# Attention's projected blocks in another order, and the last six units of the last pattern interleaved differently on TensorE

## The chip, the core and the metric

The kernel runs on one core of one Trainium2 chip. The metric is the device time of one execution in microseconds (us). A core has a matrix engine (TensorE, PE in the profile, with its weight loads as PEld), a vector engine (VectorE, DVE), a scalar engine (ScalarE, ACT), GpSimd (POOL) and a queue engine (SyncE, SP) from which most DMA transfers are issued. Each engine works through its own instruction queue in order; semaphores tie the queues together.

## The reference, cut to what matters

A trunk of two layers on 1024 tokens of width 1024: attention and a gated feed-forward network, then an RWKV-7 time mix and another feed-forward network. Only the attention of the first layer is touched. It projects the normed tokens to sliding-window heads (12 query heads on 3 key/value heads, window 128, with a sink) and to three dilated patterns of 4 heads each:

```python
proj = h @ w_in + b_in
qa, ka, va, qb, kb, vb = jnp.split(proj, IN_SPLITS, axis=-1)
qa = rope_partial(...); ka = rope_partial(...)
out_a, _ = banded_attention(qa, ka, va, A_WINDOW - 1, sinks)
for gi, (win, dil) in enumerate(((128, 1), (512, 4), (2048, 16))):
    o, l = dilated_attention(qb[:, :, gi], kb[:, :, gi], vb[:, :, gi], win, dil)
wts = jax.nn.softmax(jnp.stack(lses), axis=0)
out_b = jnp.sum(wts[..., None] * jnp.stack(outs), axis=0)
return jnp.concatenate([out_a, out_b], axis=-1) @ w_out
```

`banded_attention` takes blocks of 128 queries, each against its own and the block before, with a softmax. In the last pattern a block of 128 queries sees only its own 128 keys.

## The kernel before

Every float32 product is done as three matmuls on a value split into a high and a low part (`split`, `load_split`, `mm3`, lines 149 to 176): ACT casts the high part, DVE subtracts it to get the low part, both at line 154.

The projection is cut into 24 blocks of 128 output columns, listed in `PROJ` (line 41): `ak01` and `ak2` are the keys of the sliding heads (two, and the third), `aq`, `q`, `k`, `v` with a group number 0 to 2 and a pair number 0 or 1 are queries of the sliding heads and queries, keys and values of the patterns. A block is done in two halves of 512 tokens. `project` runs one half: 8 steps of 3 matmuls (24 matmuls of 128x512), handing control back after the third, the sixth and the last step. A half ends in an eviction: `rotated` (rotary embedding through ACT, DVE, POOL and DVE), `window_keys`, or `values` (an ACT eviction to `vT`, line 360, whose transposes on PE are put in the list `late` and done later by `transpose_values`, with an ACT copy to `vt`, line 350).

The attention itself is cut into 48 units, a unit being 128 queries of 4 heads: 8 units for each of the windows 0, 1, 2 (`window`) and of the patterns 0, 1, 2 (`pattern`). A unit (`unit`, line 439 on) has three steps. Step 0: scores (PE, line 454, tiles `sc`), the mask with the row minimum (DVE, line 458) and four exponentials (ACT, line 466) into the tile `pr`; the windows also divide by the sum there (DVE and POOL, line 473). Step 1: transposes on PE (line 481, tiles `tr`) and two ACT copies to `pT` (line 483). Step 2: values times probabilities on PE (line 490, one PSUM tile `pv`) and a DVE copy into the output tile (line 492: `oa` for the windows, `ob` for the patterns). The scores use two PSUM tiles for one unit, so the next unit's scores wait for this unit's DVE pass.

The order on PE is written out by hand: `seen` chains every one of these matmuls to the one before. The loop of lines 538 to 552 goes through the 48 half-blocks. In each it starts one unit if the block number has reached that unit's number in `todo` (step 0 ahead of the matmuls, the unit before gets its step 1 after the first part and its step 2 after the second) and does one pending value transpose behind each of these. With the numbers of before, unit steps begin at the ninth half-block, so that 40 units start within the loop and the 8 units of pattern 2 are left. What is left runs in a second loop (lines 553 to 560), two deep: the scores of one unit, then steps 1 and 2 of the unit before. The queues of the other engines are laid out by the scheduler that builds the program.

After each four units of a window its `oa` tile is written to memory (`oT`, line 528); after a pattern's last unit its `ob` goes to `oB` (line 506) and its sums to `st`. `oT` is read back (`oraw`, line 622) into the buffers of the projection's weights and split (line 154, tiles `o`) into the memory of the normed tokens `hx`, so these casts wait for the last matmuls that read `hx`. Then `out_proj` loads `wout` (line 167), while `merge` reads `oB` (tiles `om`, line 606) and weighs the patterns.

Of the kernel before, what the change touches and what calls it, by code (L numbers as in the profile page):

```python
# [11 lines left out]
F32 = mybir.dt.float32  # L12
# [9 lines left out]
P = 128  # L22
# [5 lines left out]
H = 512  # L28
# [9 lines left out]
VNAMES = ["nm0", "nf0", "nm1", "nf1", "mu0", "mu1", "mu2", "mu3", "mu4", "mu5", "w0", "a0", "kk", "ka", "rk", "lb"]  # L38
VI = {n: i for i, n in enumerate(VNAMES)}

PROJ = ["ak01", "ak2"] + [f"{n}{i}{pr}" for n, i in (("aq", 0), ("k", 0), ("q", 0), ("aq", 1), ("k", 1), ("v", 1), ("q", 1), ("aq", 2),
                                                     ("k", 2), ("v", 2), ("q", 2)) for pr in range(2)]
NV = 448


# [34 lines left out]
def lay_out(inp):  # L80
# [16 lines left out]
    for p in range(3):  # L97
        for pr in range(2):
            for n, c in (("aq", 0), ("q", 1152), ("k", 1920), ("v", 2688)):
                sl[f"{n}{p}{pr}"] = two(c + 256 * p + P * pr)  # L100
    o["win"] = np.stack([w[:, sl[n]].reshape(NK, P, P).transpose(1, 0, 2).reshape(P, NK * P) for n in PROJ])
    o["bin"] = np.stack([b[sl[n]] for n in PROJ], 1)
    v0 = np.concatenate([np.arange(2688, 2944), np.arange(960, 1152)])
# [19 lines left out]
class Trunk:  # L123
# [137 lines left out]
    def attention(self, hp, mp):  # L261
# [82 lines left out]
        late = []  # L344
# [81 lines left out]
        ap = pool("ap", 2)  # L426
# [12 lines left out]
        def unit(q, kT, keys, mask, vs, stat, sink, dst):  # L439
# [5 lines left out]
            n = keys.stop - keys.start  # L445
# [1 line left out]
            nm, den = stat if stat else (ap.tile([P, 4], F32, name=n_, tag=n_, bufs=6) for n_ in ("am", "ad"))  # L447

            ss = [psum.tile([P, 2, 256], F32, name="sc", tag="sc") for _ in range(2)]
            p = ap.tile([P, 4, 256], F32, name="pr", tag="pr", bufs=2)  # L450
            for pr in range(2):
                for e in range(2):
                    r = slice(e * 64, e * 64 + 64)
# [62 lines left out]

        def window(j, b, state):
            if b % 4 == 0:
                state[:] = [ap.tile([P, 2, H], F32, name="oa", tag="ol", bufs=2)]
            os_ = state[0]  # L520
            kb = [0] if b == 0 else [b - 1, b]
            yield from unit([qw[j][:, pr, b * P:(b + 1) * P] for pr in range(2)], [kTA[:, j]] * 2, slice(kb[0] * P, (b + 1) * P),
                            maskA[:, P:] if b == 0 else maskA, [[vtA[:, i, j * 64:(j + 1) * 64]] * 4 for i in kb], None,
                            slice(4 * j, 4 * j + 4), os_[:, :, b % 4 * P:(b % 4 + 1) * P])
            if b % 4 == 3:
                q = b // 4
                for pr in range(2):
                    nc.sync.dma_start(oT[2 * j + pr][:, q * H:(q + 1) * H], os_[:, pr])
            yield
# [1 line left out]


        todo = []
        for of, j, n in ((window, 0, 4), (pattern, 0, 8), (window, 1, 10), (pattern, 1, 16), (window, 2, 18), (pattern, 2, 24)):
            state = []
            todo += [(of(j, b, state), n) for b in range(NB)]
        before = None
        for at in range(2 * len(PROJ)):
            i = at // 2
            if at % 2 == 0 and 2 <= i + 1 < len(PROJ):  # L540
                weights(i + 1)
            mm = project(i, at % 2, seen)
            here = todo.pop(0)[0] if todo[0][1] <= i else None
            for part in range(3):
                if here and part == 0:
                    next(here)
                if before and part:
                    next(before)
                if late and part:
                    transpose_values(*late.pop(0))  # L550
                next(mm)
            before = here
        for here, _ in [*todo, (None, 0)]:
            if here:
                next(here)
            if late:
                transpose_values(*late.pop(0))
            for _ in range(2):
                next(before)
            before = here  # L560
        ev = mp.tile([P, 8, 3, 4], F32, name="ev")
        selr = mp.tile([44, 6 * P], F32R, name="selr")
        two = (slice(0, 12), slice(32, 44))
# [1068 lines left out]
```

## Time and profile before

| what | us |
|---|---|
| median of three runs (lowest, highest) | 2867.52 (2865.66, 2872.91) |
| the profiled execution | 2867.93 |
| its span, first to last instruction | 2866.2 |
| busy PE, DVE, ACT, POOL | 2674.2, 1789.1, 1204.6, 1099.7 |
| loop over the half-blocks, about 90 to 463.6 | 373.6, PE busy 371.25 |
| the units after it, 463.6 to 513.7 | 50.1, PE busy 31.95 |
| from there to the first matmul of the output projection | 12.8, PE busy 0 |

Times in the trace count from the first instruction of the span. The execution's own time is 1.7 us longer than its span. PE is busy for 93% of the span as a whole, but not in every stage, so a stage is read from the rows of its own stretch: how busy each engine is there, the clock that was granted to PE (1.00 is full speed), and what ended each idle time of PE.

### The profile page before, as it was taken

To read this page: it belongs to the slowest core of one execution; us is meant where nothing else is said; L and a number is where in the kernel's file an instruction comes from. 1 tells how busy PE (TensorE), PEld (TensorE's weight loads), DVE (VectorE), ACT (ScalarE), POOL (GpSimd) and SP (SyncE) were. 2 spreads that over 40 slices of the span, in tenths; PEclk is the share of its full clock that TensorE was granted. 3 is DMA by queue.
4 is the path that set the end of the run, shared out by engine and by line. 5 is a ranking of instruction groups with operands and counts; after the bars stand their busy time and mean duration, and the time that the engine had idled before them with its cause. 6 is when DMAs were issued, how large, how long until landed. Compare 5 with 4: busy or idle time off the path is not lost. (4 is left out here: it accounts for less than half of the span.)

```text
span 2866.2 us, 38024 instructions
## 1 busy us (share of the span) xinstructions
PE 2674.2 (93%) x13302; PEld 2135.3 (75%) x13302; DVE 1789.1 (62%) x3017; ACT 1204.6 (42%) x2377; POOL 1099.7 (38%) x830
## 2 busy tenths in 40 slices
PE   8999997799999999998899889888899999999998
PEld 6777775577888877786577667777787888887776
DVE  4555555457444437798667888767676544444988
ACT  3445444234333334355544454434334433333334
POOL 1221211136443424545444433334643534431644
PEclk9999997799999999999999999789999999999999
DMA  4111111452222227462446366787743222225654
GB/s 138 38 45 46 45 51 46 150 191 78 83 82 78 85 94 263 151 207 78 154 138 166 98 212 163 195 216 208 208 162 129 89 89 77 85 70 184 217 155 162
DMA packets 301536, 367.18 MB, mean 128 GB/s; under 512 B 101000, under 2 KB 175112, under 8 KB 301344
## 3 DMA queue, kind: packets, MB, share of 16 engines
q1 hardware_dynamic: 296560, 351.08, 39.5%
q10 hardware_dynamic: 4496, 12.62, 1.1%
q8 instruction: 105, 1.72, 0.3%
q0 software_dynamic: 288, 1.05, 0.1%
q14 instruction: 87, 0.71, 0.1%
HBM read 268.98 MB, written 95.68 MB: 127 GB/s over the span
## 5 line engine op out<-in xcount | busy, mean ns | idle before, releaser
L910 PE MATMUL pd<-ws,as 128*128 128x512 f32 x1848 | 435.7, 397 | 19.9 <-DVE ws L154 18.8
L910 PEld LDWEIGHTS pd<-ws,as 128*128 128x128 f32 x1848 | 353.5, 192 | 100.0 <-DVE ws L154 23.9
L762 PE MATMUL y<-t,cw 128*128 128x512 f32 x1584 | 370.2, 389 | 0.0
L762 PEld LDWEIGHTS y<-t,cw 128*128 128x128 f32 x1584 | 297.3, 188 | 62.4
L154 DVE TENSOR_TENSOR cw<-raw,cw 128x512 fp32r<-128x512 f32 x264 | 214.5, 815 | 197.2 <-ACT cw L154 195.9
L154 ACT CAST cw<-raw 128x512 fp32r<-128x512 f32 x264 | 163.4, 621 | 242.5 <-PE z L762 102.3
L154 ACT CAST wh<-raw 128x512 fp32r<-128x512 f32 (+1 forms) x154 | 119.8, 780 | 202.5 <-PE mm L174 58.4
L154 DVE TENSOR_TENSOR wl<-raw,wh 128x512 fp32r<-128x512 f32 (+1 forms) x146 | 144.0, 988 | 95.2 <-ACT wh L154 94.9
L771 POOL TENSOR_TENSOR c<-c 128x512 f32<-128x512 f32 x66 | 111.4, 1688 | 188.1 <-DVE c L778 137.0
L173 PE MATMUL mm<-hx,wh 128*128 128x512 f32 x384 | 163.3, 425 | 0.0
L766 ACT COPY sn<-y 128x512 f32<-128x512 f32 x132 | 77.0, 588 | 196.4 <-PE y L762 193.1
L175 PE MATMUL mm<-hx,wl 128*128 128x512 f32 x384 | 152.3, 397 | 0.0
L174 PE MATMUL mm<-hx,wh 128*128 128x512 f32 x384 | 151.6, 395 | 0.0
L762 PE MATMUL z<-b,cw 128*128 128x512 f32 x576 | 141.6, 396 | 6.6 <-DVE tx L708 6.6
L257 POOL TENSOR_TENSOR ry<-ry,S 128x512 f32<-128x512 f32 x40 | 52.0, 1301 | 222.5 <-DVE ry L256 198.0
L154 ACT CAST as<-raw 128x512 fp32r<-128x512 f32 x110 | 68.3, 621 | 157.4 <-PE pd L910 82.3
L762 PEld LDWEIGHTS z<-b,cw 128*128 128x128 f32 x576 | 110.2, 192 | 30.8 <-issue 7.0
L762 PE MATMUL y<-b,cw 128*128 128x512 f32 x528 | 129.0, 394 | 0.0
L762 PE MATMUL z<-t,cw 128*128 128x512 f32 x528 | 123.3, 389 | 0.0
L804 POOL TENSOR_TENSOR raw<-s,raw 128x512 f32<-128x512 f32 x44 | 59.9, 1362 | 152.8 <-DVE cw L154 152.6
L762 PE MATMUL x<-b,cw 128*128 128x512 f32 x480 | 117.4, 400 | 0.0
L154 DVE TENSOR_TENSOR as<-raw,as 128x512 fp32r<-128x512 f32 x110 | 100.0, 909 | 27.4 <-ACT as L154 27.3
(469 smaller groups left out, 6122.5 us busy)
## 6 DMA issues: line engine op xcount, KB each, us to landing
raw<-act SPq DMA_DIRECT2D x132, 256.0 KB, 3.5
raw<-in_wd SPq DMA_DIRECT2D x132, 256.0 KB, 3.3
raw<-in_wg SPq DMA_DIRECT2D x88, 256.0 KB, 2.9
raw<-in_wu SPq DMA_DIRECT2D x88, 256.0 KB, 2.5
act<-c SPq DMA_DIRECT2D x88, 256.0 KB, 2.0
raw<-in_wrk SPq DMA_DIRECT2D x32, 512.0 KB, 4.6
raw<-in_win SPq DMA_DIRECT2D x24, 512.0 KB, 3.3
raw<-in_wout SPq DMA_DIRECT2D x32, 256.0 KB, 3.8
```

Of the source, the lines that this page charges most:

```text
L154: return self.nc.scalar.copy(hi, src), (eng or self.nc.vector).tensor_tensor(lo, src, hi.bitcast(F32), SUB)
L173: seen(mm(ps, lh, rh, start=start, stop=False))
L174: seen(mm(ps, lh, rl, start=False, stop=False))
L175: seen(mm(ps, ll, rh, start=False, stop=stop))
L257: nc.gpsimd.tensor_tensor(y, y, self.S[:, s], MUL)
L762: seen(pe.matmul(ps, w[:, x, s], bs[:, k, y], start=start and k == j == 0, stop=k == 3 and j == 2, skip_group_check=True))
L766: ac.copy(s, ps)
L771: po.tensor_tensor(g, g, u, MUL)
L804: po.tensor_tensor(a11, s, a11, SUB)
L910: pe(ps[b], s[:, x, t], w[:, y], start=first and i == 0, stop=f == N - 1 and i == 2, skip_group_check=True)
```

## The change

Three things change. `PROJ` has another order: `ak2` comes just ahead of window 2's queries instead of second, and `v2` behind `q2`. The numbers in `todo` follow it: window 0 starts at block number 3, counted from 0 (the seventh half-block), and two units of pattern 2 start in the last two half-blocks, so that 42 units start in the loop and 6 are left; the last half-block skips its step 2. The remaining units run three deep: a turn has the scores of unit u, step 2 of unit u-3 and step 1 of unit u-2 (unit 0 gets its step 2 in the first turn). To hold this, `pr` has three buffers instead of two, and `oa` one instead of two. Because `v2` is now the last block, the transposes of its second pair fall behind the loop.

```diff
-PROJ = ["ak01", "ak2"] + [f"{n}{i}{pr}" for n, i in (("aq", 0), ("k", 0), ("q", 0), ("aq", 1), ("k", 1), ("v", 1), ("q", 1), ("aq", 2),
-                                                     ("k", 2), ("v", 2), ("q", 2)) for pr in range(2)]
+two_of = lambda *names: [f"{n}{pr}" for n in names for pr in range(2)]
+PROJ = ["ak01", *two_of("aq0", "k0", "q0", "aq1", "k1", "v1", "q1"), "ak2", *two_of("aq2", "k2", "q2", "v2")]
...
-            p = ap.tile([P, 4, 256], F32, name="pr", tag="pr", bufs=2)
+            p = ap.tile([P, 4, 256], F32, name="pr", tag="pr", bufs=3)
...
-                state[:] = [ap.tile([P, 2, H], F32, name="oa", tag="ol", bufs=2)]
+                state[:] = [ap.tile([P, 2, H], F32, name="oa", tag="ol", bufs=1)]
...
-        for of, j, n in ((window, 0, 4), (pattern, 0, 8), (window, 1, 10), (pattern, 1, 16), (window, 2, 18), (pattern, 2, 24)):
+        for of, j, n in ((window, 0, 3), (pattern, 0, 7), (window, 1, 11), (pattern, 1, 15), (window, 2, 19), (pattern, 2, 23)):
...
-                if before and part:
+                if before and (part == 1 or part == 2 and at + 1 < 2 * len(PROJ)):
                     next(before)
...
+            last_two = before, here
             before = here
-        for here, _ in [*todo, (None, 0)]:
-            if here:
-                next(here)
-            if late:
+
+        live = [[u, n] for u, n in zip(last_two, (2, 1))] + [[u, 0] for u, _ in todo]
+
+        def step(u, n):
+            if 0 <= u < len(live) and live[u][1] == n:
+                next(live[u][0])
+                live[u][1] += 1
+
+        for u in range(2, len(live) + 3):
+            step(u, 0)
+            while late:
                 transpose_values(*late.pop(0))
-            for _ in range(2):
-                next(before)
-            before = here
+            step(u - 3, 2)
+            step(u - 2, 2)
+            step(u - 2, 1)
```

How it moves instructions is seen at two places. The first is TensorE behind the last projection matmul. `sc` are scores, `tr` transposes of probabilities, `tq` transposes of values, `pv` the products with the values (`vtA` the windows', `vt` the patterns'). Before:

```order
L454 MATMUL sc<-kT,q 128x128 x4
L481 MATMUL tr<-cst,pr 128x128 x8
L490 MATMUL pv<-pT,vtA 64x128 x8
L454 MATMUL sc<-kT,q 128x128 x4
L481 MATMUL tr<-cst,pr 128x128 x4
L490 MATMUL pv<-pT,vt 64x128 x4
```

And with the change:

```order
L454 MATMUL sc<-kT,q 128x128 x4
L349 MATMUL tq<-cst,vT 128x128 x8
L490 MATMUL pv<-pT,vt 64x128 x4
L454 MATMUL sc<-kT,q 128x128 x4
L481 MATMUL tr<-cst,pr 128x128 x4
L454 MATMUL sc<-kT,q 128x128 x4
L490 MATMUL pv<-pT,vt 64x128 x4
L481 MATMUL tr<-cst,pr 128x128 x4
L454 MATMUL sc<-kT,q 128x128 x4
L490 MATMUL pv<-pT,vt 64x128 x4
```

The last window unit's transposes and products have moved into the loop, two groups of value transposes have come out of it, and the transposes of a unit now stand two scores behind its own, with a further unit's scores between them and their products.

The second place is ScalarE at the same time, from the casts of the window outputs (`o<-oraw`) on. Before:

```order
L154 CAST o<-oraw 128x512 x6
L254 ACTIVATE rx<-mm,bias 128x512
L154 CAST o<-oraw 128x512 x4
L466 ACTIVATE pr,stat<-pr,stat 128x128 x4
L483 COPY pT<-tr 128x512 x2
L466 ACTIVATE pr,stat<-pr,stat 128x128 x3
L483 COPY pT<-tr 128x256
L466 ACTIVATE pr,stat<-pr,stat 128x128
L483 COPY pT<-tr 128x256
L154 CAST o<-oraw 128x512 x2
```

And with the change:

```order
L154 CAST o<-oraw 128x512 x6
L360 ACTIVATE vT<-mm,bias 128x64x8
L154 CAST o<-oraw 128x512 x3
L350 COPY vt<-tq 128x4x128
L154 CAST o<-oraw 128x512
L466 ACTIVATE pr,stat<-pr,stat 128x128 x4
L154 CAST o<-oraw 128x512 x2
L350 COPY vt<-tq 128x4x128
L466 ACTIVATE pr,stat<-pr,stat 128x128
L483 COPY pT<-tr 128x256
L466 ACTIVATE pr,stat<-pr,stat 128x128
L483 COPY pT<-tr 128x256
```

The eviction of the last value block and its two copies now stand among the twelve casts, ahead of the first exponentials of the remaining units; all twelve casts stand ahead of the first copy of `pT` there.

More of the change, by code (lines that the diff above doesn't have):

```diff
@@ L551, in attention @@
                 next(mm)
+            last_two = before, here
             before = here
-        for here, _ in [*todo, (None, 0)]:
-            if here:
-                next(here)
-            if late:
+        live = [[u, n] for u, n in zip(last_two, (2, 1))] + [[u, 0] for u, _ in todo]
[6 more added lines that the diff above has]
+            while late:
                 transpose_values(*late.pop(0))
-            for _ in range(2):
-                next(before)
-            before = here
+            step(u - 3, 2)
+            step(u - 2, 2)
+            step(u - 2, 1)
+        assert all(n == 3 for _, n in live)
         ev = mp.tile([P, 8, 3, 4], F32, name="ev")
```

## The prediction

> **What bounds the kernel now.** I read the granted clock in the page's slices first, then the time by stretch, then TensorE's rows around the weakest stretch.
>
> ```profile
> PEclk9999997799999999999999999789999999999999
> ```
>
> Each digit is a fortieth of the span, 71.7 us. Slices seven and eight (430 to 573) are the weakest. The change lies there, so I cut that time into the loop over half-blocks, the units behind it, and the wait for the output projection. The columns are the length, the busy time of PE, PEld, DVE, ACT and POOL with counts, the granted clock, the DMA share and GB/s.
>
> ```profile
> 90.00:463.60 373.60, 371.25 (x2239) 278.29 (x2238) 203.71 (x643) 178.86 (x499) 79.47 (x60) 1.00 0.14 46
> 463.60:513.70 50.10, 31.95 (x185) 20.80 (x184) 22.41 (x88) 23.50 (x91) 2.40 (x3) 0.57 0.11 33
> 513.70:526.50 12.80, 0.00 (x0) 0.00 (x0) 2.98 (x11) 0.90 (x2) 1.70 (x4) 0.50 0.90 274
> ```
>
> The loop is PE-bound: 2.35 us idle in 373.6. Behind it no engine is: 50.1 us in which PE is busy for 31.95 at 0.57 of its clock, ACT for 23.5, DVE for 22.4. That is a chain of waits, and PE's rows show which.
>
> ```profile
> 472.57 0.80 PE L454 MATMUL sc<-kT,q 64*128 64x128 f32 x4 [8.47 <-DVE q L333]
> ...
> 483.52 1.11 PE L481 MATMUL tr<-cst,pr 128*128 128x128 f32 x4
> ...
> 505.58 1.34 PE L490 MATMUL pv<-pT,vt 128*64 128x128 f32 x8 [1.00 <-ACT pT L483]
> 506.85 1.23 PE L454 MATMUL sc<-kT,q 64*128 64x128 f32 x8
> 508.01 1.11 PE L481 MATMUL tr<-cst,pr 128*128 128x128 f32 x4
> 510.12 1.35 PE L490 MATMUL pv<-pT,vt 128*64 128x128 f32 x8 [1.00 <-ACT pT L483]
> 511.40 1.12 PE L481 MATMUL tr<-cst,pr 128*128 128x128 f32 x4
> 512.55 1.12 PE L490 MATMUL pv<-pT,vt 128*64 128x128 f32 x8
> 526.51 0.79 PE L173 MATMUL po<-wh,o 128*128 128x512 f32 x1 [12.84 <-ACT wh L154]
> ```
>
> First 8.47 us wait for the rotated `q` of the very last block. Then each unit takes 4.54 us (505.58 to 510.12): scores 1.16, transposes about 1.1, a wait, products 1.28, all at half clock. At the end 12.84 us until the first weights of the output projection are split.
>
> **The change, part by part.**
>
> *The wait for `q` goes.* `q2` now ends at half-block 44 and the two first units of pattern 2 start at 47 and 48. The last block is `v2`, which no score reads.
>
> *The loop grows.* It takes in two score steps, one four-matmul transpose step and the last window unit's steps 1 and 2, and gives up the two transpose groups of the last value pair. Full-clock prices:
>
> ```profile
> 457.33 1.04 PE L481 MATMUL tr<-cst,pr 128*128 128x128 f32 x8
> 458.12 0.48 PE L173 MATMUL mm<-hx,wh 128*128 128x512 f32 x1
> ...
> 460.40 0.66 PE L490 MATMUL pv<-pT,vtA 128*64 128x128 f32 x8
> 461.42 0.66 PE L490 MATMUL pv<-pT,vtA 128*64 128x128 f32 x8 [0.36 <-ACT pT L483]
> 462.01 0.50 PE L173 MATMUL mm<-hx,wh 128*128 128x512 f32 x1
> 462.34 0.39 PE L174 MATMUL mm<-hx,wh 128*128 128x512 f32 x1
> 462.57 0.39 PE L175 MATMUL mm<-hx,wl 128*128 128x512 f32 x1
> ```
>
> Eight transposes take 0.79 (457.33 to 458.12), a window's products 1.25 (460.40 to 462.01 less 0.36), scores half of 1.16. So 2 x 0.58 + 0.40 + 0.79 + 1.25 - 2 x 0.40 = 2.8 us. The distance between a block's rotation and its first reader elsewhere is as before or longer, so I put no new stall there; up to one more 2.35 us as bound.
>
> *The units behind the loop.* With three deep, a unit's exponentials have a whole turn of PE's to run in, and ACT's queue becomes the longest work. Its prices:
>
> ```profile
> 461.27 3.22 ACT L154 CAST o<-oraw 128x512 fp32r<-128x512 f32 x6
> 473.79 0.40 ACT L466 ACTIVATE pr<-pr,stat 128x128 f32<-128x128 f32 x1 [5.85 <-DVE stat L458]
> 475.35 1.04 ACT L483 COPY pT<-tr 128x512 f32<-128x512 f32 x2
> 480.69 0.35 ACT L483 COPY pT<-tr 128x256 f32<-128x256 f32 x1
> 480.94 0.40 ACT L466 ACTIVATE pr<-pr,stat 128x128 f32<-128x128 f32 x1
> 483.64 1.25 ACT L154 CAST o<-oraw 128x512 fp32r<-128x512 f32 x2 [1.96 <-DMA oraw<-oT]
> ```
>
> ```profile
> L360 ACT ACTIVATE vT<-mm,bias 128x512 f32<-128x512 f32 x8 | 9.4, 1174 | 6.6 <-PE mm L175 6.6
> ```
>
> Four exponentials take 1.56 (473.79 to 475.35), a cast 0.54 (3.22 for six), a 512-wide copy 0.52 (1.04 for two), two 256-wide copies 0.6 (0.25 and 0.35), the eviction of `vT` 1.17. Let E be the end of the last projection matmul. The first six casts wait for the last reader of half of `hx`, 12 matmuls of 0.23 before E: they run from E-2.8 to E+0.4. Then, in the built order: eviction of `vT` to 1.6, three casts 3.2, first `vt` copy 3.7, cast 4.2, unit 2's exponentials 5.8, two casts 6.9, second `vt` copy 7.4. The value transposes on PE wait for these (one `tq` tile), so PE stands idle some 3 of the first 4 us. From there each of units 3 to 7, counted from 0, brings its exponentials and the copies of the unit two before it, 1.56 + 0.6 = 2.16: 18.2. Behind that are the products of unit 5 (half a window's, 0.6), then for units 6 and 7 transposes 0.4, copies 0.6 and products 0.6 at full clock: E+22.0. DVE had a little less to do than ACT in this stretch (22.41 against 23.50), so it does not set the end. This is the lower bound.
>
> The upper bound is PE at half clock, never waiting from 3.7 on: 1.1 for the second value transposes, five scores at 1.16, five transposes at 1.11, five products at 1.28, so 22.6; then unit 5's products with the copy ahead of them 1.5 and two last pairs of 2.27 (511.40 to 513.67): E+28.6.
>
> Which one depends on the granted clock. These stretches are each as long as the shortest one at full clock, 484.86 to 488.27; the columns are PE's busy time, the clock and the DMA share, and the last two are from a later stage:
>
> ```profile
> 478.03:481.45 3.42, 2.47 (x16) 0.50 0.40 153
> 481.45:484.86 3.41, 3.19 (x20) 0.53 0.47 154
> 484.86:488.27 3.41, 0.62 (x6) 0.97 0.00 0
> ```
>
> ```profile
> 1996.95:2000.36 3.41, 1.66 (x15) 1.00 0.82 236
> 2000.36:2003.78 3.42, 2.22 (x26) 1.00 0.74 246
> ```
>
> Busy for 0.62 of 3.41, PE falls to half; busy for 2.47, it stays there; after 3.19 it rises; and once up, 1.66 of 3.41 (49%) did not lower it. So the idle start probably drops the clock, but at half clock PE is then busy without a gap, which raises it within two such stretches, by about E+10, and from there the 1.6 us that a unit takes at full clock (0.58 + 0.40 + 0.63) in each 2.16 (74%) hold it. While it is low, ACT is behind anyway. I take E+23.0, near ACT's end.
>
> ```profile
> 478.43 0.80 SPq L528 DMA_DIRECT2D oT<-oa  x2
> 480.52 0.90 SPq L622 DMA_DIRECT2D oraw<-oT  x2
> ...
> 520.64 0.99 SPq L167 DMA_DIRECT2D raw<-in_wout  x2
> ```
>
> *The read-back.* All window outputs are now written before E; before, the last went out at 478.43, was read back at 480.52 and made ACT wait 1.96 at 483.64.
>
> ```profile
> raw<-in_win SPq DMA_DIRECT2D x19, 512.0 KB, 3.3
> oB<-ob POOLq DMA_DIRECT2D x2, 512.0 KB, 6.3
> ```
>
> *The 12.84 us behind the tail.* SP's queue reads `st`, then `om`, then loads `wout`; the fourth `om` waits for POOL's two writes of the last `ob`, 6.3 us, which share the DMA engines (0.90 busy) with three `om` reads. Now the last unit's sums are ready two drain pairs before the end, so these reads go out before the writes begin. Between nothing and 3.0 (6.3 against 3.3 for one such transfer alone) I take 1.7, since two writes still share.
>
> **Sum.** +2.8 (loop) + 23.0 - 50.1 (units) - 1.7 (weights) = -26.0 against the profiled 2867.93, which is 0.4 above the median 2867.52: 2841.9, and 2841.5 beside the median. I say 2842. Ends: 2.8 + 22.0 - 50.1 - 3.0 = -28.3, so 2839.6; 2.8 + 2.35 + 28.6 - 50.1 = -16.3, so 2851.6. What follows is serial on the attention's result and PE-bound, so it shifts.
>
> **The rivals.**
>
> *The clock stays low to the end:* E+28.6, so 2867.9 + 2.8 + 28.6 - 50.1 - 1.7 = 2847.5. For it: the tail of before never stayed up. Against: there PE had about 1 us of idle in each stretch (3.42 - 2.47), and here it would have none. The Trainium skill, TensorE: Matmul & The Clock Gate, in its section on PE-mode transpose, says that transposes do not count as busy for the gate. By that rule a third of this tail would not count and the clock would stay low; the trace disagrees, since the stretch at 481.45 rose with the transposes of 483.52 among its 3.19 us.
>
> *The casts and their reads hold ACT:* every exponential, copy and so PE stands behind them. Once more the 1.96 us of 483.64, and the 1.7 not gained: 2845.6. For it: all six transfers fall around E. Against: the last window output is written a half-block earlier.
>
> *The loop pays:* 42 units with the 0.36 us wait of 461.42 each would be 15.1 us: 2857. Against: the loop had 40 units and 2.35 us idle in all.
>
> *Slower: the single `oa` buffer.* The next unit's DVE copy must wait for `oT` to be read out, and behind it on DVE stand masks and rotations, so PE.
>
> ```profile
> 159.79 0.42 DVE L492 COPY oa<-pv 128x256 f32<-128x256 f32 x1
> ```
>
> ```profile
> 150.92 0.80 SPq L528 DMA_DIRECT2D oT<-oa  x2
> 163.47 0.33 SPq L167 DMA_DIRECT2D raw<-in_win  x1
> ```
>
> The write is out 2.1 us after its issue (478.43 to 480.52), 6.8 us before the copy. If a weight load that waits for its buffer stood ahead of it on SP, it would go at 163.8 and land at 165.9: 6.1 us for each of three windows, 18 in all, 2860. Two loads ahead, one more gap of 12.5: 56 us, 2898. It makes the kernel slower from 8.7 us per window on. The built order has the write where it was, so this is unlikely.
>
> **How the numbers follow.** The forecast has 0.58, the low clock 0.18, the casts 0.13, the loop 0.06, the single buffer 0.05 (0.03 with one load ahead, 0.02 with two). The range, 2837 to 2852, holds the forecast's own ends and the first two rivals; its low end allows the loop's 2.35 us of idle to go as well. A measurement here tells 0.3% (8.6 us) from no change: faster 0.95 (the first four), the same 0.03 (2860 is 7.5 below the median), slower 0.02.
>
> **What would show it.** PE's 8.47 us wait for `q` at line 333 gone; the loop's end about 3 us later, near 466; between it and the last `pv` 22 to 25 us, idle mostly in the first 4; ACT without long waits for `stat` there; the clock back at 1.00 before the last units; SP's `om` reads issued before POOL's writes, and under 12 us to the first `po`. I am wrong if the tail stays above 30 us, or if idle of PE in the loop grows by more than 3.

## The result and the profile after

The changed kernel took 2835.31 us (median of four runs, 2833.78 to 2844.29), the kernel before 2870.22 us (median of four, 2865.66 to 2875.29). The ratio is 0.9887, with a 95% interval of 0.9868 to 0.9905: 27 to 38 us faster. The forecast was 2842; the measured time is 6.7 us under it and 1.7 us under the low end of the range. Four more runs of the same kernel, taken later, gave 2836.86 us and a ratio of 0.9876 (0.9852 to 0.9900). Ratios here and below are of fast runs; of the kernels below, deep_only had one slow run of 6543.09 us, which its ratio leaves out and its median of 2867.61 holds (2867.32 without it).

The profiled execution of the changed kernel is one of its slower ones (2844.29 us), so its whole length says less than its stages. Its page, span and granted clock by slices:

```profile
span 2842.5 us, 38023 instructions
PEclk9999999999999999999999899789999999999999
```

The two slices of 7 at the seventh and eighth place of before are gone. The same three stretches as before, loop, units and wait (the columns are the length, busy time of PE, PEld, DVE, ACT and POOL with counts, granted clock, DMA share, GB/s):

```profile
90.00:466.05 376.05, 374.05 (x2274) 280.11 (x2273) 207.89 (x667) 183.02 (x518) 81.60 (x63) 1.00 0.14 47
466.05:487.56 21.51, 15.55 (x149) 10.38 (x148) 14.81 (x64) 18.72 (x72) 0.00 (x0) 1.00 0.20 54
487.56:500.75 13.19, 0.01 (x2) 0.01 (x1) 3.00 (x11) 0.90 (x3) 1.70 (x4) 0.65 0.80 255
```

The loop is 2.45 us longer and PE idles 2.00 us in it. The units take 21.5 us instead of 50.1, at a clock of 1.00 instead of 0.57, and ACT is busy for 18.7 of them. The wait in front of the output projection is 13.2 us, no shorter than the 12.8 of before. PE's rows in these stretches, with the waits in brackets:

```profile
466.05 0.71 PE L454 MATMUL sc<-kT,q 64*128 64x128 f32 x8
467.45 0.66 PE L349 MATMUL tq<-cst,vT 128*128 128x128 f32 x4 [0.69 <-ACT vT L360]
469.82 0.66 PE L349 MATMUL tq<-cst,vT 128*128 128x128 f32 x4 [1.72 <-ACT vt L350]
470.41 0.66 PE L490 MATMUL pv<-pT,vt 128*64 128x128 f32 x8
...
481.65 0.71 PE L490 MATMUL pv<-pT,vt 128*64 128x128 f32 x8 [0.36 <-ACT pT L483]
...
486.85 0.71 PE L490 MATMUL pv<-pT,vt 128*64 128x128 f32 x8 [0.30 <-ACT pT L483]
500.75 0.79 PE L173 MATMUL po<-wh,o 128*128 128x512 f32 x1 [13.18 <-ACT wh L154]
```

There is no wait for `q` any more. ACT's rows of the same time have hardly a gap from the eviction of `vT` to the last exponential of the last unit (the longest is 0.33 us, for the read of an `oraw`, ahead of the cast at 468.67):

```profile
466.25 1.15 ACT L360 ACTIVATE vT<-mm,bias 128x512 f32<-128x512 f32 x1
...
472.76 0.58 ACT L350 COPY vt<-tq 128x512 f32<-128x512 f32 x1
473.24 0.41 ACT L466 ACTIVATE pr<-pr,stat 128x128 f32<-128x128 f32 x1
...
481.24 0.62 ACT L483 COPY pT<-tr 128x256 f32<-128x256 f32 x2
481.76 0.40 ACT L466 ACTIVATE pr<-pr,stat 128x128 f32<-128x128 f32 x1
...
482.94 0.39 ACT L466 ACTIVATE pr<-pr,stat 128x128 f32<-128x128 f32 x1
...
483.57 0.36 ACT L483 COPY pT<-tr 128x256 f32<-128x256 f32 x1
484.83 0.65 ACT L483 COPY pT<-tr 128x256 f32<-128x256 f32 x2 [0.90 <-PE tr L481]
```

The first matmul of the output projection starts at 500.75 instead of 526.51: 25.8 us earlier, where 26.0 was forecast. So the place of the change gave what was worked out for it as a total, and the 33 to 35 us between the medians hold something besides. That is the question that the experiments had to settle.

A part of it shows 1350 us later. The second layer has a recurrence on PE; its products `o<-sb,bm` mark its first and its last start, and the time between the two is called the recurrence's length below (the row gives the shortest, median and longest duration in ns, then first and last start). Before:

```profile
L1495 PE MATMUL o<-sb,bm x256: 275/275/377, 1879.8 to 2097.9; 128*128 128x128 f32 x128
```

and with the change:

```profile
L1504 PE MATMUL o<-sb,bm x256: 275/275/377, 1859.8 to 2072.6; 128*128 128x128 f32 x128
```

218.1 us became 212.8, in code that the change doesn't touch. The queues of the engines are laid out by the scheduler that builds the program, and it put this stage in another order: on PE the first instructions that differ behind the attention are in the projections ahead of the recurrence, and in it POOL's updates of the state `S`, the norm of `y` and the additions to `vn` alternate otherwise. With 25.8 us ahead of the output projection this makes 31.1 us, inside both intervals. These two profiles alone don't add up to it: from the first matmul of the output projection to the end they took 2339.7 us before and 2341.7 with the change, so that in this slower execution the other stages behind took back more than the 5.3.

### The profile page after: what moved, and what is told of

It reads as the page before. It is cut to its first block, busy times and chain, and to the rows that moved or that the text cites. A ratio compares the mean times of both kernels' runs of the same rounds, so it can differ in the third digit from the quotient of the medians.

```text
span 2842.5 us, 38023 instructions
## 1 busy us (share of the span) xinstructions
PE 2660.4 (94%) x13302; PEld 2123.9 (75%) x13302; DVE 1781.8 (63%) x3017; ACT 1203.2 (42%) x2377; POOL 1101.3 (39%) x830
## 3 DMA queue, kind: packets, MB, share of 16 engines
q1 hardware_dynamic: 296560, 351.08, 40.2%
## 5 line engine op out<-in xcount | busy, mean ns | idle before, releaser
L787 DVE TENSOR_TENSOR c<-z,sn 128x512 f32<-128x512 f32 x92 | 63.4, 689 | 84.8 <-ACT sn L775 74.4
```

What stands on the lines that cost most here:

```text
L787: ve.tensor_tensor(c[-1], z, s, ADD)
```

## The experiments

Times of stages are from one profile of each kernel; the time and the ratio to the kernel before are from the timed runs. Each ratio is against runs of the kernel before taken beside it (medians of 2865 to 2870 us), so the ratios compare across rows better than the times. "Tail" is from the end of the last projection matmul to the end of the last product, "wait" from there to the first output-projection matmul (`po`).

| kernel | time, us | ratio (95%) | tail | wait | first `po` | recurrence |
|---|---|---|---|---|---|---|
| before | 2870.22 | 1 | 50.0 | 12.8 | 526.5 | 218.1 |
| changed | 2835.31 | 0.9887 (0.9868 to 0.9905) | 21.4 | 13.2 | 500.7 | 212.8 |
| again | 2836.86 | 0.9876 (0.9852 to 0.9900) | 21.2 | 12.6 | 501.2 | 212.7 |
| order_only | 2844.82 | 0.9917 (0.9894 to 0.9940) | 32.2 | 12.2 | 510.5 | 214.1 |
| deep_only | 2867.61 | 0.9988 (0.9977 to 0.9999) | 37.2 | 12.7 | 514.7 | 229.6 |
| om_pool | 2833.47 | 0.9874 (0.9849 to 0.9898) | 21.0 | 10.1 | 496.6 | 214.1 |
| pt_dve | 2852.70 | 0.9945 (0.9924 to 0.9966) | 20.6 | 12.4 | 499.2 | 230.0 |
| cast_pool | 2839.25 | 0.9899 (0.9878 to 0.9919) | 19.3 | 13.1 | 498.4 | 219.3 |
| w_best | 2835.19 | 0.9885 (0.9867 to 0.9903) | 21.6 | 4.5 | 492.2 | 218.8 |
| before_orderA | 2863.46 | 0.9981 (0.9971 to 0.9991) | 50.0 | 12.0 | 529.5 | 213.1 |
| after_orderD | 2846.39 | 0.9924 (0.9908 to 0.9941) | 24.3 | 11.9 | 506.2 | 217.4 |
| w_best_orderA | 2832.63 | 0.9877 (0.9855 to 0.9899) | 23.2 | 5.2 | 496.0 | 211.8 |
| pt_dve_orderB | 2846.67 | 0.9921 (0.9907 to 0.9935) | 23.2 | 13.2 | 504.6 | 219.7 |
| best | 2831.02 | 0.9868 (0.9853 to 0.9883) | 19.4 | 9.8 | 494.8 | 214.1 |

**The same kernel once more (again).** No edit.

> The changed kernel once more, nothing edited. First theory: the change is worth what its profile shows up to the first matmul of the output projection, 526.51 - 500.75 = 25.8 us, and what follows only shifts, so five rounds give a ratio near 0.991 (26 of 2868). Rival: the stages behind it gain as well, since its timed runs of 2834 to 2836 lie some 9 us under the profiled one; then the ratio stays at 0.988 and the part from the first output-projection matmul to the end, 2341.7 us in the first profile and 2339.7 before, is nearer 2332 here. Up to that matmul the profile should repeat within 1 us: loop to 466.1, last product at 487.6, first output-projection matmul near 500.7.

Up to the first `po` the profile repeated within 1.3 us, and the recurrence within 0.1. From that matmul to the end it took 2334.4 us where the first profile had 2341.8, with the recurrence equal: one execution can differ from the next by 7 us in the other stages, and the timed runs of this kernel span 2828 to 2844. The ratio stays at 0.988, so the first theory (only 25.8 us, nothing behind) is the weaker one. The medians differ by 33 to 35 us, 7 to 9 more than 25.8; the recurrence's 5.3 is the one part of it that both profiles show, and the rest is within what runs differ by.

**The new order with a two-deep tail (order_only).** The tail's loop is the old one, on the new `PROJ` and `todo`:

```diff
-        for u in range(2, len(live) + 3):
+        for u in range(2, len(live) + 1):
             step(u, 0)
...
-            step(u - 3, 2)
             step(u - 2, 2)
-            step(u - 2, 1)
+            step(u - 1, 1)
+            step(u - 1, 2)
```

> The new block order and unit numbers alone: the last six units run two deep as before (scores of unit u, then steps 1 and 2 of unit u-1). The loop ends at 466.1 as in the changed kernel and the 8.47 us wait for q is gone. First theory: the order is most of the gain, because a two-deep unit at full clock needs 0.58 + 0.40 + 1.0 (the wait for pT) + 0.63 = 2.6 us, PE is busy for 62% of it and the clock stays at 1.00; seven such units behind the value transposes end about 25 us behind the last projection matmul, against 21.5 with three deep, so 3 to 4 us slower than the change. Rival: only three deep keeps PE busy enough; the clock falls to a half, a unit takes 4.54 us as before, and the units end about 36 us behind the last projection matmul, 14 us slower than the change.

The tail took 32.2 us, between the two. Three rows of its stretches, each as long as the shortest at full clock (columns as above):

```profile
470.93:474.34 3.41, 1.39 (x19) 0.91 (x17) 2.01 (x4) 2.53 (x9) 0.00 (x0) 1.00 0.00 0
474.34:477.75 3.41, 2.56 (x18) 1.42 (x14) 1.21 (x9) 2.18 (x10) 0.00 (x0) 0.50 0.00 0
487.99:491.41 3.42, 2.41 (x14) 1.30 (x12) 0.93 (x8) 2.18 (x10) 0.00 (x0) 0.50 0.02 5
```

PE was busy for 1.39 of 3.41 (41%) in one stretch, the next had half the clock, and it stayed there until the last product was done. The longest idle time of that stretch is one wait of 2.02 us, which the profile puts down to DVE's low parts of the casts (`o`, line 154). From then on PE's rows show about the old period of 4.54 us, with the old wait:

```profile
473.25 0.71 PE L490 MATMUL pv<-pT,vt 128*64 128x128 f32 x8 [2.02 <-DVE o L154]
...
485.59 1.35 PE L490 MATMUL pv<-pT,vt 128*64 128x128 f32 x8 [0.90 <-ACT pT L483]
...
490.14 1.35 PE L490 MATMUL pv<-pT,vt 128*64 128x128 f32 x8 [1.01 <-ACT pT L483]
```

So the order alone is worth 16.0 us up to the first `po`, and three deep another 9.7 on top of it. Three deep buys less idle time, and with it the clock: PE idled 8.7 us in this tail and 6.0 in the changed kernel's, and the same matmuls kept it busy for 23.4 us at a mean clock of 0.63 against 15.5 at 1.00. The rival was right on the clock, the first theory on the order being most of the gain.

**Three deep with the old order (deep_only).** The kernel before, with three `pr` and one `oa` buffer, and this loop for its eight remaining units:

```diff
-        for here, _ in [*todo, (None, 0)]:
...
+        live = [[before, 1]] + [[u, 0] for u, _ in todo]
...
+        for u in range(1, len(live) + 3):
+            step(u, 0)
+            while late:
+                transpose_values(*late.pop(0))
+            step(u - 3, 2)
+            step(u - 2, 1)
```

> The old block order and unit numbers with the eight remaining units three deep (three pr buffers, one oa buffer as in the change). The 8.47 us wait for q stays at the start and the clock falls to a half there, as before. First theory: behind the wait PE is busy without gaps at half clock for about two windows of 3.4 us, the clock rises, and then ACT sets 2.16 us per unit: 8.5 + 7 + 6 x 2.16 + 3 = 31.5 us for the stretch that took 50.1 before, so some 18 us faster than before, and 7 to 10 slower than the whole change. Rival: the clock stays at a half, PE needs 3.5 us per unit, 8.5 + 8 x 3.5 + 3 = 40 us, 10 us faster than before only.

The tail is 37.2 us, nearer the rival's 40 than 31.5. The wait for `q` is there, as both said, and a second one comes in the middle, on ACT for the read-back of the last window outputs, with PE behind it:

```profile
473.68 0.80 PE L454 MATMUL sc<-kT,q 64*128 64x128 f32 x4 [8.46 <-DVE q L333]
...
487.23 0.70 PE L490 MATMUL pv<-pT,vt 128*64 128x128 f32 x4 [2.56 <-ACT pT L483]
```

```profile
486.29 0.62 ACT L154 CAST o<-oraw 128x512 fp32r<-128x512 f32 x1 [2.12 <-DMA oraw<-oT]
```

The clock had risen before that wait and fell again during it. This is the read-back of the prediction: 1.96 us before, 2.12 here, 0.33 in the new order. Up to the first `po` the kernel is 11.8 us ahead of before; yet the time is only 0.12% lower, because its recurrence took 229.6 us, 11.5 more than before.

**The reads of pattern 2 off SP's queue (om_pool).**

```diff
-                    nc.sync.dma_start(l[g], oB[g, pr][:, q * H:(q + 1) * H])
+                    d = (nc.gpsimd if g == 2 else nc.sync).dma_start(l[g], oB[g, pr][:, q * H:(q + 1) * H])
+                    if g == 2:
+                        self.after(d, ec)
```

(`ec` is POOL's copy into `e2`, so that the read stands behind it.)

> The changed kernel, but the reads of pattern 2's outputs (the third om of each pair) are issued from POOL's queue behind its own oB writes, so that SP's loads of wout no longer stand behind a read that waits for these writes. First theory: the 13.18 us between the last product and the first output-projection matmul are set by that place on SP (raw<-in_wout goes at 496.06, behind om reads issued from 487.85 on); now they go near 489 and land in 4 us, so the first output-projection matmul comes 5 to 7 us earlier, near 494.5, and the time falls by 4 to 6 us. Rival: the DMA engines, 0.80 busy there, set it: the loads share with the oB writes and land no more than 2 us earlier, or the merge, which needs the same reads, gives the gain back later: within 2 us of the change.

In the changed kernel's SP and POOL queues the loads of `wout` stand behind an `om` read that waits for POOL's writes:

```profile
485.96 0.37 SPq L579 DMA_DIRECT2D mtmp<-st  x1
486.38 0.57 SPq L615 DMA_DIRECT2D om<-oB  x1
...
487.85 8.12 SPq L615 DMA_DIRECT2D om<-oB  x4
496.06 1.04 SPq L167 DMA_DIRECT2D raw<-in_wout  x2
```

In this kernel they went at 488.17:

```profile
486.83 1.29 SPq L615 DMA_DIRECT2D om<-oB  x3
488.17 0.92 SPq L167 DMA_DIRECT2D raw<-in_wout  x2
```

The loads were issued 7 us sooner relative to the last product, but the wait fell only from 13.2 to 10.1: they now go out together with the two `oB` writes, and the DMA engines are busy for 0.96 of the wait instead of 0.80. Both theories hold in part, and the time (2833.47) cannot be told from the changed kernel's.

**One pT copy on DVE (pt_dve).**

```diff
-                nc.scalar.copy(pTs[-1][:, :nk * 256], pt[:, :nk * 256])
+                (nc.vector.tensor_copy if nk == 1 and pr else nc.scalar.copy)(pTs[-1][:, :nk * 256], pt[:, :nk * 256])
```

> The changed kernel, but where a unit has one key block only (all of pattern 2) the second of its two pT copies is done by DVE instead of ACT. First theory: ACT's work sets the 21.5 us behind the loop (ACT has no gap from 466.25 to 483.9); 0.3 us less for each of eight units, so the last product ends 19 to 20 us behind the last projection matmul, 1.5 to 2.4 us sooner. Rival: the chain of one unit through PE, DVE and ACT sets it, and the copy on DVE stands behind row minima there: no change or up to 2 us longer.

The tail shrank by 0.9 us, about half of what was expected: ACT lost its load, but now it waits for DVE's row minima in turn, as the rival said:

```profile
478.74 0.40 ACT L466 ACTIVATE pr<-pr,stat 128x128 f32<-128x128 f32 x1 [0.17 <-DVE stat L458]
...
480.93 0.40 ACT L466 ACTIVATE pr<-pr,stat 128x128 f32<-128x128 f32 x1 [0.29 <-DVE stat L458]
```

The whole kernel is 17 us slower than the change, though its first `po` comes 1.6 us sooner. The recurrence took 230.0 us:

```profile
L1504 PE MATMUL o<-sb,bm x256: 274/275/582, 1850.1 to 2080.1; 128*128 128x128 f32 x128
```

**Six of the twelve casts on POOL (cast_pool).**

```diff
-                self.split(os2[q][k // 4][:, k % 4, 0], os2[q][k // 4][:, k % 4, 1], raws[6 * q + k])
+                hi, lo = (os2[q][k // 4][:, k % 4, i] for i in range(2))
+                (nc.gpsimd.tensor_copy if q else nc.scalar.copy)(hi, raws[6 * q + k])
+                nc.vector.tensor_tensor(lo, raws[6 * q + k], hi.bitcast(F32), SUB)
```

> The changed kernel, but the high parts of six of the twelve window outputs (the second half of the tokens) are cast by POOL instead of ACT. First theory: the casts ahead of the units' exponentials hold ACT; 6 x 0.54 = 3.2 us leave it, PE's wait of 1.72 for the value copy and the waits for pT in the first units go, and the last product ends near 18.5 us behind the last projection matmul, 3 us sooner. Rival: the start is set by the chain of the last value block (eviction, transposes, copy, transposes) and DVE's low parts, which now wait for POOL's casts ahead of row minima: less than 1 us sooner or even longer.

The tail is 2.1 us shorter (19.3), between the two theories: two thirds of the casts' 3.2 us came out. ACT's load ahead of the units is therefore on the path, and with pt_dve's 0.9 us this bears out that ACT sets the tail, with DVE close behind. The time is no better than the changed kernel's, and the recurrence, 219.3 us, is again another.

**The wout load ahead of the sums (w_best).** The edit of om_pool, and the read of `st` behind the first load on SP:

```diff
+        self.loaded = self.nc.sync.dma_start(raw[:p], src)
...
-            nc.sync.dma_start(ms, st.rearrange("(b p) g e -> p b g e", p=P))
+            self.after(nc.sync.dma_start(ms, st.rearrange("(b p) g e -> p b g e", p=P)), self.loaded)
```

> The edit of om_pool, and besides the read of the sums st stands behind the first load of wout on SP, so that this load goes as soon as its buffer is free (a row minimum of the last units, near 482.3). First theory: it lands near 486.5, is cast behind the last pT copies, and the first output-projection matmul follows the last product within 2 us instead of 13.18; the first 12 matmuls then run at full clock in 2.8 us, and PE waits some 4 us more for the merge's sums (ev was ready at 492.2), so that 7 to 9 us remain: near 2827. Rival: the merge's chain, sums to om to the split o, sets the end of this stage whatever stands ahead of it, and less than 3 us remain.

The wait fell from 13.2 to 4.5 us, and the median did not move. PE's next wait is for the low part of the same weight, and DVE, which makes it, stood behind the sums; their read, moved behind a load of 256 KB and in between POOL's writes, now landed only at 496.05:

```profile
492.15 0.80 PE L173 MATMUL po<-wh,o 128*128 128x512 f32 x1 [4.53 <-ACT wh L154]
496.90 0.79 PE L174 MATMUL po<-wl,o 128*128 128x512 f32 x1 [3.95 <-DVE wl L154]
```

```profile
496.05 0.19 DVE L580 TENSOR_TENSOR mtmp<-mtmp 128x32 f32<-128x32 f32 x1 [7.39 <-DMA mtmp<-st]
```

From the first `po` to the first matmul of the next down projection it took 549.9 us where the changed kernel took 547.5 and 545.3, so 2.4 to 4.6 of the 8.6 came back there; the recurrence took back 6 (218.8).

**Which order, not which edit.** Comparing the built programs from the second layer on, instruction by instruction on all five engines, these kernels fall into five orders:

| order of the second layer | kernels and recurrence, us |
|---|---|
| A | changed 212.8, again 212.7, order_only 214.1, om_pool 214.1 |
| B | before 218.1 |
| C | deep_only 229.6, pt_dve 230.0 |
| D | cast_pool 219.3 |
| E | w_best 218.8 |

Within an order the recurrence repeats to 1.4 us; between orders it differs by up to 17. But the kernels of one order also have other things in common. So three experiments were meant to move the order alone. All add fifteen small instructions with no effect on the result, here on POOL:

```diff
         ev = mp.tile([P, 8, 3, 4], F32, name="ev")
+        nc.gpsimd.memset(ev, 0.0)
+        nc.gpsimd.tensor_copy(ev, ev)   # fourteen times
```

Before, brought to order A (before_orderA):

> The kernel before, with its attention as it was, and fifteen small POOL instructions (a memset and fourteen 128x96 copies of ev onto itself, overwritten later) behind it. Their only purpose is to move the scheduler: on all five engines the order of the second layer behind them is then the one that the changed kernel has, row for row. First theory: the recurrence of the second layer (first to last product of sb) takes what it took in the four profiles with this order, 212.7 to 214.1 us, instead of 218.1, so the part from the first output-projection matmul to the end loses about 5 us though nothing of the attention changed; first output-projection matmul at 526 to 528; time 3 to 6 us under the kernel before. Rival: the length of the recurrence is set by the clock of the run or by when it starts, not by the order: 218 us, and no gain.

```profile
L1510 PE MATMUL o<-sb,bm x256: 275/275/377, 1879.3 to 2092.4; 128*128 128x128 f32 x128
```

213.1 us, as expected, and a ratio of 0.9981 (0.9971 to 0.9991), 2.6 to 8.3 us under the kernel before, with its attention as slow as it was.

The changed kernel, brought to order D (after_orderD):

> The changed kernel with the same fifteen small POOL instructions. Here they move the scheduler away from the order of the changed kernel, to the one that the kernel with six casts on POOL had, row for row. First theory: first output-projection matmul near 501 as in the changed kernel, recurrence near 219.3 us instead of 213, time 5 to 7 us over the changed kernel (near 2841). Rival: nothing but the clock of the run: 213 us and 2835.

The recurrence took 217.4 us, 4.6 more than with order A; the time rose by 10, because the first `po` came 5.0 us later as well, some of it in a later end of the loop (470.1 instead of 466.1 to 467.4) and 3 us in the tail, where the clock fell to half for two stretches of 3.41 us (mean 0.86). That part was not expected: the added instructions are not free in this kernel, so the timed runs don't show what the order is worth here.

The kernel of pt_dve, brought to order B with the fourteen copies on ACT (pt_dve_orderB):

> The kernel with the second pT copy on DVE, and fifteen small instructions (a memset on POOL and fourteen 128x96 copies of ev onto itself on ACT, overwritten later), which only move the scheduler: the order of the second layer is then that of the kernel before instead of the one that this kernel shared with deep_only. First theory: the 17 us by which pt_dve was slower than the change lie in that order, so the recurrence takes 218 us instead of 230.0 and the time falls by about 12 us, to 2841 or so, while the units behind the loop stay at 20.6 us and the first output-projection matmul at 499. Rival: the DVE copies cost it, or what follows them; the recurrence stays near 230 us and the time near 2853.

```profile
L1519 PE MATMUL o<-sb,bm x256: 275/275/582, 1851.9 to 2071.6; 128*128 128x128 f32 x128
```

219.7 us instead of 230.0; the time fell by 6 and not by 12, since here too the first `po` comes later, by 5.5 us: the loop ends 2.0 us later, and the tail, its clock at half for three such stretches (mean 0.78), takes 2.7 us more. The DVE copies were not what made pt_dve slow.

In all three the length went where the order says. Two things limit what follows from it. Orders A and D part only ahead of the recurrence: from 1590 us on, the traces of the changed kernel, cast_pool and after_orderD have the same rows in the same sequence on PE, DVE, ACT and POOL and the same transfers on SP (by the program's names, without buffer numbers). So between these two it isn't the recurrence's own rows that stand otherwise. And its first product can come sooner or later than the rest of its stage. From the first `pv<-wh,xi`, ahead of the projections (1307.2 before, 1286.5 with the change), to the last `o<-sb,bm` it took 772.5 to 786.1 us in seven profiles with the recurrence of order A, 786.1 and 780.6 of them in the two of the changed kernel. It took 790.7 and 783.0 in B, 785.9 and 788.4 in D, 782.8 in E, 791.5 and 797.2 in C. By this longer stretch C is slower than A, and each of the others overlaps A. The gain of order A over B that is timed, on a kernel whose attention is no faster, is before_orderA's 2.6 to 8.3 us.

What in the order costs the time, the stretches show only by kind (columns as above; before, changed and pt_dve):

```profile
1879.80:2097.90 218.10, 182.58 (x1441) 160.65 (x1441) 156.56 (x308) 82.31 (x183) 116.11 (x94) 0.96 0.74 203
```

```profile
1859.80:2072.60 212.80, 182.81 (x1441) 160.49 (x1441) 155.24 (x308) 82.52 (x183) 115.50 (x94) 0.96 0.76 206
```

```profile
1850.10:2080.10 230.00, 189.77 (x1440) 166.95 (x1441) 157.50 (x309) 82.18 (x183) 117.65 (x94) 0.92 0.71 192
```

The work is the same to a few instructions. PE idles 35.5 us before, 30.0 with the change and 40.2 in pt_dve, and there the clock is lower too (0.92), with PE busy 7 us longer on the same matmuls. Which of the moved rows does it was not tried and stays open.

**Towards a better kernel.** w_best_orderA is w_best with the three pieces of the first merge behind the weights 0, 2 and 4 instead of 0, 1 and 2:

```diff
-                        if merged and k in ((0, 1, 2), (0, 1, 2))[c]:
+                        if merged and k in ((0, 2, 4), (0, 1, 2))[c]:
```

> The edit of w_best, and the three pieces of the first merge stand behind the weights 0, 2 and 4 of the output projection instead of 0, 1 and 2, so that PE has 24 matmuls and not 12 ahead of the first row of the merge that needs pattern 2's outputs; the order of the recurrence is then that of the changed kernel. First theory: first output-projection matmul near 492.2 as in w_best, recurrence 213 to 214 us, and so 2835 - 8.6 = 2826 or a little less. Rival: the merge's reads arrive no sooner, and PE waits for them behind the 24 matmuls: 2830 or more.

2832.63 us, nearer the rival. Its profile has the end of the last projection matmul 1.5 us and the last product 3.3 us later than the changed kernel's, and the part from the first `po` to the next down projection is 550.7 us, 3 to 5 longer than the changed kernel's: PE still waits 2.97 us for the low part behind the sums. Its tail ran at a mean clock of 0.85. The recurrence was as short as expected (211.8); its order is the changed kernel's but for a few rows near 1911 us.

best joins om_pool, cast_pool and the wider spacing of the merge, in order A:

> The edits of om_pool and cast_pool together, and the three pieces of the first merge behind the weights 0, 2 and 4, with which the order of the recurrence is the changed kernel's. First theory: 2.1 us less in the units behind the loop (19.3), 3.1 us less up to the first output-projection matmul (10.1), so that one near 496; recurrence 213 to 214 us; time 5 us under the changed kernel, 2830. Rival: the merge takes the 5 us back, as it did with w_best, where the first matmul came 8.6 us sooner and the median did not move: 2834 to 2836.

```profile
494.77 0.80 PE L173 MATMUL po<-wh,o 128*128 128x512 f32 x1 [9.81 <-ACT wh L154]
```

The first `po` comes at 494.8, the recurrence takes 214.1, and the median of 2831.02 is the lowest of all. The forecast of 2830 was near; but its interval (0.9853 to 0.9883) overlaps that of the changed kernel, so that it beats the kernel before is shown, that it beats the change is likely and not shown.

## Why the prediction was right, and where not

**The wait for `q` goes: right.** No row of PE waits for line 333 behind the loop, and deep_only, with the old order, keeps 8.46 us of it.

**The loop grows by 2.8: right.** The last projection matmul ends 2.45 us later (466.12 against 463.67), and PE's idle time in the loop went from 2.35 to 2.00 us. The 0.36 us waits of that rival did not spread.

**The units take 23.0 behind the last projection matmul: the mechanism was right, the size 1.6 too large.** They took 21.4, just under the stated lower end of 22.0. The larger part, 1.0, is the step from that lower end to the forecast, which was there for a low clock at the start; the clock stayed at 1.00. The other 0.6 lies in the lower end itself, spread thin: ACT's queue was at 7.2 behind the last matmul instead of 7.4, the five units' exponentials and copies behind it took 10.6 instead of 10.8 (to 483.93; the exponentials follow each other in 0.39 us), and the drain 3.6 instead of 3.8. ACT as the bound is borne out by cast_pool, where 3.2 us less of casts gave 2.1; pt_dve adds that DVE is close behind, which the sum had taken from one total (22.41 against 23.50) only.

**"The idle start probably drops the clock": wrong, without harm.** PE idled 2.4 us at the start and not some 3, and in the weakest stretch of the tail it was busy for 1.69 of 3.41 us (50%), with the clock still 1.00 in the next:

```profile
467.66:471.07 3.41, 1.69 (x18) 1.00 0.59 203
471.07:474.48 3.41, 2.79 (x24) 1.00 0.00 0
```

(Here the second figure is PE's busy time alone, then the clock, the DMA share and GB/s.) Both profiles of the changed kernel have 1.00 through the whole tail, so the upper end, with PE at half clock throughout, and the rival of the low clock did not come true there. But it was a near thing, and not by the row order alone: w_best has the same rows in the same sequence on PE, ACT and DVE in its tail, and its clock fell to half for one stretch (w_best_orderA, with the same rows too, for two):

```profile
471.26:474.67 3.41, 2.49 (x21) 1.00 0.44 128
474.67:478.08 3.41, 3.41 (x23) 0.50 0.00 0
```

Of the ten three-deep tails with the new block order, six kept 1.00 and four fell for one to three stretches; the two-deep one fell and stayed low. The prediction's own stretches lay 0.23 us behind the clock's steps: laid on the step at 484.63, PE was busy for 3.41 of 3.41 ahead of the rise (not 3.19) and 0.45 ahead of the fall (not 0.62).

The Trainium skill, TensorE: Matmul & The Clock Gate, in its section on PE-mode transpose, says of TensorE's transpose mode that it doesn't count as PE-busy in the same way. The rows don't say whether this kernel's transposes use that mode. About 1.0 of the 1.69 us in that stretch are the transposes of 467.45 and 469.82, so some 0.65 of other matmuls are left, and the clock held; order_only's stretch of 1.39 us has 0.3 us of transposes, so 1.1 of others, and the clock fell. These two stretches speak against the rule, as far as two can.

**"SP's `om` reads go out before POOL's writes begin", worth 1.7 us: wrong.** The wait grew by 0.34 us instead. The reads did go out a little earlier against the writes: three of the four reads in the row of 487.85 were issued in its first microsecond, around POOL's first write at 488.54 (before, the row began at 514.90, behind the write at 514.65). But the path doesn't run through them. POOL issues the writes 0.98 us behind the last product in both kernels, SP's fifth read (the prediction has the fourth) waits for them, and the `wout` loads stand behind it, at 496.06. That wait on SP was 6.5 us, where the longest before was 4.0; why the writes took longer is open. om_pool shows that the place in the queue is worth 3.1 us. w_best, whose first load goes ahead of POOL's writes, has a wait of 4.5, which fits that sharing the DMA engines with them costs about half of the rest.

**The casts and their reads: right that the reads would not hold ACT.** It waited 0.33 us for one, against 1.96 before and 2.12 in deep_only. The casts' own time is on the path, as cast_pool shows, and the sum had it there.

**The single `oa` buffer: no stall showed.** The loop's idle time did not grow. It was not tried apart.

**"What follows is serial on the attention's result and PE-bound, so it shifts": wrong, and this is the miss in the total.** The place of the change gave 25.8 us against 26.0 forecast; that it came so near is luck, with the units 1.6 better, the loop 0.35 better and the wait 2.0 worse than the sum. Of the 7 to 9 us beyond, 5.3 are the recurrence by its marks, in an order that the scheduler chose anew, and before_orderA gives that order 2.6 to 8.3 us by timed runs. The rest, 2 to 4 us, is not traced to a stage. The comparison of the two orders of the whole program would have shown, ahead of the run, that the second layer's rows move; it would not have told the sign.

## What to carry to other kernels

Where a scheduler lays out the queues, an edit is two changes: the one that was written, and a new order of everything behind it. Compare the order of the whole program, split a measured gain by stages, and repeat a surprising result with an edit that moves only the order: here the recurrence's length moved by -6 to +12 us, as much as most of the edits tried were worth.

A chain of waits in a short stage costs twice, once as idle time and once as clock. Going from two deep to three shortened the tail by 10.7 us; 2.8 of them were PE's idle time, and the rest was the same matmuls at a mean clock of 1.00 instead of 0.63. A stage that sits near the edge can fall over it for reasons that the sequence of its own rows doesn't show, as w_best did.

A transfer that stands behind a waiting one on an in-order queue is not freed by making the writer earlier, if reader and writer move together. It needs another queue or another place, and what is moved behind it (here the sums) must be priced as well.

## What the runs showed that was not expected

The same 1441 matmuls of the recurrence took 211.8 to 230.0 us in fourteen profiles, sorted by the order of the whole layer: 211.8 to 214.1 in order A, 217.4 to 219.7 in B, D and E, 229.6 and 230.0 in C. That A and D differ, though the rows from 1590 us on don't, is unexplained.

What lowers the clock is not a plain share of busy time as the profile counts it. Stretches of 3.41 us with 0.45 and 1.39 us busy were followed by half clock and one of 1.69 was not, but one of 1.76 us in deep_only was, and so was w_best's of 2.49. A stretch of 3.41 us busy at half clock raised it in deep_only, where another in order_only did not:

```profile
475.72:479.13 3.41, 3.41 (x19) 0.50 0.03 7
479.13:482.54 3.41, 3.28 (x42) 1.00 0.20 77
482.54:485.96 3.42, 1.76 (x18) 1.00 0.67 213
485.96:489.37 3.41, 2.14 (x11) 0.50 0.04 17
```

```profile
481.17:484.58 3.41, 3.41 (x20) 0.50 0.00 0
484.58:487.99 3.41, 2.51 (x17) 0.50 0.00 0
```

The ends of matmuls are modelled, and the stretches were laid on the clock's steps to within some hundredths of a microsecond. No line between busy times that hold the clock and busy times that lose it fits all of these stretches.
